# Splitting the last stores of a local-attention kernel, and issuing half of the very last one earlier

## The chip, the cores and the metric

One core of a Trainium2 chip. It has four compute engines (TensorE, VectorE, ScalarE and GpSimd: PE, DVE, ACT and POOL in the views) and SyncE (SP), which waits and issues transfers. Data are moved by 16 DMA engines; a packet of the trace is one piece that one of them moves, mostly one partition's share of a transfer (a unit's store shows 128 packets of 24,576 bytes, eight on each DMA engine). A semaphore is a counter that engines and transfers raise and that others wait for. The metric is device time in microseconds (us) of one execution; times named "of the trace" count from the start of the profiled span, which is about 2 us shorter than the device time (941.3 against 943.3).

## The reference, cut to what matters

```python
B, S, D, W = 4, 4096, 1536, 64            # float32 q, k, v and output, 100.66 MB each
# in windows of 64 rows, no row sees another window:
logits = einsum('bnwd,bnud->bnwu', q_w, k_w) * D ** -0.5
attn   = softmax(logits)
out    = einsum('bnwu,bnud->bnwd', attn, v_w)
```

Per input byte there is little arithmetic: each window is read once and written once.

## The kernel before

The 16,384 rows are worked off in N = 32 units of 512 rows; a partition holds four rows of a unit. GpSimd issues the loads (but for the first q, which SyncE loads) and the stores of units 0 to 30 on one queue; SyncE issues the very last store on its own queue. GpSimd's loads turn float32 into 16 bits on the way, so the packets count fewer bytes (253 MB) than HBM (403 MB); the page gives such a load of a unit 1536 KB, its store 3072. Three output buffers go round, so unit u may write its buffer when the store of unit u - 3 has landed.

```python
def store(u):                                          # GpSimd, one transfer of 3 MB
    nc.gpsimd.dma_start(
        out=rows(of, u * UR, SLOTS, SLOTS), in_=slots(outs[u % NO], 0, SLOTS, SLOTS)
    ).then_inc(d_o[u % NO], 16)
# ...
def told(ins, u, n, j, a):                             # n: row 0 to 3, j: third of the row
    if u == N - 1 and n >= 2:
        ins.then_inc(n_e[a], 1)                        # the last unit's rows 2 and 3 report here
    else:
        ins.then_inc(f_o[j][n], 1)
# ...
for u in range(1, N):                                  # GpSimd's stream
    hand_over("q", u, q16, m_q, g_q)                   # wait for the load, copy, request unit u + 2
    hand_over("k", u, k16, m_k, g_k)
    gp.wait_ge(m_q, u + 1)
    store(u - 1)
    hand_over("v", u, v16, m_v, g_v)
# SyncE, at the end:
for a in range(2):
    sy.wait_ge(n_e[a], 3)                              # VectorE's 3 and ScalarE's 3 tiles of rows 2, 3
sy.dma_start(
    out=rows(of, (N - 1) * UR, SLOTS, SLOTS), in_=slots(outs[(N - 1) % NO], 0, SLOTS, SLOTS)
).then_inc(d_l, 16)
# ... waits for all stores, then the end
```

The softmax here doesn't subtract the row's maximum and nothing guards it: scores larger than these inputs give would overflow.

## Time and profile before

| | before |
|---|---|
| time, median of 6 runs | 943.33 us (942.95 to 944.28) |
| span of the profiled run | 941.3 us |
| TensorE, ScalarE, GpSimd, VectorE busy | 68, 36, 35, 31% |
| packets of the GpSimd queue, share of 16 DMA engines | 99.7% |
| last store: issue, last packet's end, last semaphore count | 929.24, 939.46, 939.94 |

Read it as a kernel that streams: the DMA engines are full throughout (nines in the page's DMA row in all of the 40 slices but the last, which has a 7), so only the first and the last microseconds can hold idle DMA time.

How the packets lie on one DMA engine is in no view; it was worked out from the packet records of the trace, by chaining each packet to the one that ends where it starts. Two of the 16 chains of the tail, in us (an ordinary listing, not a view):

```
a typical engine:  ... 8 packets of the unit-30 store end 928.15 | idle 1.98 | 8 packets of the last store 930.14 to 937.50
the latest engine: ... 8 packets of the unit-30 store end 931.61 | idle 0.01 | 8 packets of the last store 931.62 to 939.46
                       (among the latter an 8 KB instruction fetch at 933.43, 0.31 long, the packet after it 1.18 instead of 0.91)
```

### The profile page before, as it was taken

The numbers are of one execution on the slowest core, as the hardware profiler recorded it, in microseconds if no ns is written. First come the engines' busy times: TensorE is split into PE (matmuls) and PEld (weight loads), VectorE is DVE, ScalarE is ACT, GpSimd is POOL, SyncE is SP. The second block draws the span as 40 slices with busy tenths as digits, with TensorE's granted clock in tenths as the row PEclk, the third lists the DMA queues.
The fourth block names the chain that finished last, engine by engine and source line by source line (L and its number), as shares of the span: only waits on it lengthen the run. The fifth ranks groups of instructions, "written<-read, shape, count | busy, mean of one in ns | idle before, by whom it ended". The sixth has DMA issues, their size and how long they took to land. (4 is left out here: it accounts for less than half of the span.)

```text
span 941.3 us, 13141 instructions
## 1 busy us (share of the span) xinstructions
PE 641.9 (68%) x5120; PEld 371.9 (40%) x3584; DVE 288.4 (31%) x517; ACT 336.0 (36%) x642; POOL 334.1 (35%) x225
## 2 busy tenths in 40 slices
PE   0877777666767767768676586676866767757673
PEld 0544444432444433444233442344533444323440
DVE  0233333332323333233322233222333223322232
ACT  0344444333333233333333333333334334233331
POOL 4244433344333342333423334333343333443220
PEclk9999999998889888797888999889789789888997
DMA  9999999999999999999999999999999999999997
GB/s 257 217 216 279 264 237 282 284 279 276 233 275 283 281 281 237 266 282 282 281 245 257 283 281 282 255 246 283 283 280 264 237 284 283 280 277 230 276 320 329
DMA packets 22540, 253.35 MB, mean 269 GB/s; under 512 B 2048, under 2 KB 2048, under 8 KB 10240
## 3 DMA queue, kind: packets, MB, share of 16 engines
q0 software_dynamic: 22240, 246.95, 99.7%
q1 hardware_dynamic: 288, 6.29, 1.7%
q14 instruction: 10, 0.08, 0.0%
q8 instruction: 2, 0.03, 0.0%
HBM read 301.99 MB, written 100.66 MB: 428 GB/s over the span
## 5 line engine op out<-in xcount | busy, mean ns | idle before, releaser
L164 PE MATMUL lt<-xq,xk 128*128 128x256 f16 x1536 | 203.3, 282 | 0.0
L300 POOL COPY v<-vl 128x3072 f32<-128x3072 f32 x31 | 85.2, 2748 | 278.3 <-DMA vl<-in_v_dram 278.3
L192 PEld LDWEIGHTS <-et 128*64 128x64 f16 x512 | 40.5, 131 | 331.6 <-issue 319.4
L152 PE MATMUL tp<-ident,k 128*128 128x128 f32 x768 | 124.9, 297 | 57.9 <-PEq L218 40.5
L164 PEld LDWEIGHTS lt<-xq,xk 128*128 128x128 f16 x1536 | 153.2, 100 | 27.3
L152 PE MATMUL tp<-ident,q 128*128 128x128 f32 x768 | 107.9, 285 | 80.1 <-DVE xq L228 55.8
L112 PE MATMUL sp<-ones,et 128*64 128x1 f16 x512 | 52.6, 178 | 147.8 <-PEq L218 130.6
L152 PEld LDWEIGHTS tp<-ident,q 128*128 128x128 f32 x768 | 85.9, 145 | 120.8 <-issue 120.7
L228 ACT COPY xk<-tp 128x512 f32<-128x512 f32 x96 | 59.6, 620 | 203.2 <-ACTq L218 203.2
L152 PEld LDWEIGHTS tp<-ident,k 128*128 128x128 f32 x768 | 96.0, 152 | 75.1 <-issue 73.1
L300 POOL COPY k<-kl 128x3072 f32<-128x3072 f32 x31 | 85.2, 2748 | 103.1 <-DMA kl<-in_k_dram 103.1
L245 DVE RECIPROCAL rs<-sp 128x1 f32<-128x1 f32 x128 | 21.4, 167 | 323.8 <-DVEq L218 323.2
L300 POOL COPY q<-ql 128x3072 f32<-128x3072 f32 x31 | 85.0, 2743 | 100.0 <-DMA ql<-in_q_dram 99.9
L228 DVE COPY xk<-tp 128x512 f32<-128x512 f32 x96 | 66.5, 693 | 168.2 <-DVEq L218 168.2
L112 PE MATMUL o<-v,et 128*64 128x512 f16 x768 | 117.7, 440 | 0.0
L279 ACT ACTIVATE out<-tp,rs 128x512 f32<-128x512 f32 x64 | 44.0, 687 | 177.4 <-ACTq L218 177.4
L269 ACT ACTIVATE et<-lt,zeros 32x128 f16<-32x128 f32 x256 | 92.0, 359 | 39.4 <-ACTq L218 36.1
L228 ACT COPY xq<-tp 128x512 f32<-128x512 f32 x96 | 56.3, 586 | 126.4 <-ACTq L218 126.4
L112 PE MATMUL tp<-v,et 128*64 128x512 f16 x512 | 100.2, 468 | 0.0
L256 DVE TENSOR_SCALAR out<-o,rs 128x512 f32<-128x512 f32 x128 | 90.4, 747 | 28.6 <-DVEq L218 28.6
L228 DVE COPY xq<-tp 128x512 f32<-128x512 f32 x96 | 66.1, 688 | 83.7 <-DVEq L218 83.7
L112 PE MATMUL lt<-v,et 128*64 128x512 f16 x256 | 64.5, 479 | 0.0
(21 smaller groups left out, 217.6 us busy)
## 6 DMA issues: line engine op xcount, KB each, us to landing
out_dram<-out POOLq DMA_DIRECT2D x31, 3072.0 KB, 61.6
ql<-in_q_dram POOLq DMA_DIRECT2D x31, 1536.0 KB, 54.9
kl<-in_k_dram POOLq DMA_DIRECT2D x31, 1536.0 KB, 54.9
vl<-in_v_dram POOLq DMA_DIRECT2D x31, 1536.0 KB, 54.9
out<-in_q_dram SPq DMA_DIRECT2D x1, 3072.0 KB, 16.7
out_dram<-out SPq DMA_DIRECT2D x1, 3072.0 KB, 10.7
k<-in_k_dram POOLq DMA_DIRECT2D x1, 1536.0 KB, 17.9
v<-in_v_dram POOLq DMA_DIRECT2D x1, 1536.0 KB, 24.3
```

Source lines behind the costliest of these rows:

```text
L112: return nc.tensor.add_instruction(mybir.InstMatmult(name=nc.get_next_instruction_name(), engine=PE, ins=[low(rhs), low(w)], outs=[low(o)] ...
L152: ins = nc.tensor.transpose(tps[g % 2][:, r, j, :], pairs[:, c * P : (c + 1) * P], ident[:, :])
L164: ins = nc.tensor.matmul(lts[h][:, r, :, :], lhsT=keys(c, h, r, w), rhs=queries(c, h, w), start=(c == 0 and w == 0 and r == 0), stop=(c == ...
L192: ld = nc.tensor.ldweights(w[h], tile_position=(0, P // H * h))
L228: copy(out=dst, in_=tps[g % 2][:, :, :, :]).then_inc(f_c[g % 4], 1)
L245: ve.reciprocal(out=rs[:, n : n + 1], in_=sp[:, n : n + 1]).then_inc(n_d, 1)
L256: ins = ve.tensor_scalar_mul(scaled(u, n, j), bank(n, j), scalar1=rs[:, n : n + 1])
L269: ins = sc.activation(ets[h][s, :, :, t], lts[h][s, :, :, t], EXP, bias=zeros[s, 0:1], scale=scale)
L279: ins = sc.activation(scaled(u, n, j), bank(n, j), COPY, bias=0.0, scale=rs[:, n : n + 1])
L300: gp.tensor_copy(out=dst[:, :, :].bitcast(FP32), in_=landing[x][u % NL][:, :, :].bitcast(FP32)).then_inc(c_l, 1)
```

## The change

Its intent: the last store should not wait for the whole last unit. Half of it goes out when rows 0 and 1 are done, and the stores of units 28 to 30 go out in halves as well, so that the end is made of smaller pieces. Core of the diff (the semaphore declarations and the changed wait counts of the buffers are cut):

```diff
     def store(u):
-        nc.gpsimd.dma_start(
-            out=rows(of, u * UR, SLOTS, SLOTS), in_=slots(outs[u % NO], 0, SLOTS, SLOTS)
-        ).then_inc(d_o[u % NO], 16)
+        n = 1 if u < N - 4 else 2
+        out, in_ = (
+            x[:, 0, :].rearrange("p (i d) -> p i d", i=n)
+            for x in (rows(of, u * UR, SLOTS, SLOTS), slots(outs[u % NO], 0, SLOTS, SLOTS))
+        )
+        for i in range(n):
+            nc.gpsimd.dma_start(out=out[:, i, :], in_=in_[:, i, :]).then_inc(d_o[u % NO], 16)
@@ SyncE, at the end
-        for a in range(2):
-            sy.wait_ge(n_e[a], 3)
-        sy.dma_start(
-            out=rows(of, (N - 1) * UR, SLOTS, SLOTS), in_=slots(outs[(N - 1) % NO], 0, SLOTS, SLOTS)
-        ).then_inc(d_l, 16)
+        last = rows(of, (N - 1) * UR, SLOTS, SLOTS)[:, 0, :]
+        for i, c in enumerate((1, 3)):
+            for a in range(2):
+                sy.wait_ge(n_e[a], c)
+            sy.dma_start(
+                out=last[:, 2 * i * D : 2 * (i + 1) * D],
+                in_=outs[(N - 1) % NO][:, 2 * i : 2 * (i + 1), :].rearrange("p r d -> p (r d)"),
+            ).then_inc(d_l[i], 16)
```

The compute engines keep their instructions and their order.

More of the change, by code (lines that the diff above doesn't have):

```diff
@@ L76 @@
     d_o = [sem(f"d_o{i}") for i in range(NO)]
-    d_l = sem("d_l")
+    d_l = [sem(f"d_l{i}") for i in range(2)]
     g_q, g_k, g_v = (sem(n) for n in ("g_q", "g_k", "g_v"))
@@ L284, in store, with stored @@
     def store(u):
-        nc.gpsimd.dma_start(
-            out=rows(of, u * UR, SLOTS, SLOTS), in_=slots(outs[u % NO], 0, SLOTS, SLOTS)
-        ).then_inc(d_o[u % NO], 16)
+        n = 1 if u < N - 4 else 2
[5 more added lines that the diff above has]
+            nc.gpsimd.dma_start(out=out[:, i, :], in_=in_[:, i, :]).then_inc(d_o[u % NO], 16)
+    def stored(u):
+        return 16 * (u // NO + 1) + (0 if u < N - 4 else 16)
     def request(x, u):
@@ L357 @@
         for u in range(NO, N):
-            sy.wait_ge(d_o[u % NO], 16 * (u // NO))
+            sy.wait_ge(d_o[u % NO], stored(u - NO))
             for a in range(2):
@@ L380 @@
             last = max(u for u in range(N - 1) if u % NO == i)
-            sy.wait_ge(d_o[i], 16 * (last // NO + 1))
-        sy.wait_ge(d_l, 16)
+            sy.wait_ge(d_o[i], stored(last))
+        for i in range(2):
+            sy.wait_ge(d_l[i], 16)
         lo, hi = min(s.num for s in sems), max(s.num for s in sems)
```

## The prediction

> **What bounds the kernel now.** I read the page first, its rows of utilisation and the DMA parts, because 32 units of the same work should show at once whether an engine or the DMA is full.
>
> ```profile
> DMA  9999999999999999999999999999999999999997
> q0 software_dynamic: 22240, 246.95, 99.7%
> q1 hardware_dynamic: 288, 6.29, 1.7%
> HBM read 301.99 MB, written 100.66 MB: 428 GB/s over the span
> ```
>
> No compute engine is over 68% busy; the 16 DMA engines are full from the first slice to the last but one. The inputs and the output must cross once (302 + 101 MB), and at the 428 GB/s of the last line that is the whole span of 941 us. So compute can only matter where the DMA engines run dry: at the start and at the end. The change touches only the end, so I next read the timeline of the last 40 us, with the waits of SyncE and the issues by line.
>
> ```profile
> 902.45 2.75 POOL L300 COPY k<-kl 128x3072 f32<-128x3072 f32 x1 [4.52 <-DMA kl<-in_k_dram]
> 905.82 0.54 POOL L285 DMA_DIRECT2D out_dram<-out  x1 [0.62 <-POOL k L300]
> 917.14 2.75 POOL L300 COPY v<-vl 128x3072 f32<-128x3072 f32 x1 [10.78 <-DMA vl<-in_v_dram]
> 926.22 0.69 ACT L279 ACTIVATE out<-tp,rs 128x512 f32<-128x512 f32 x1 [1.04 <-ACTq L218]
> 927.80 1.41 DVE L256 TENSOR_SCALAR out<-o,rs 128x512 f32<-128x512 f32 x2 [0.45 <-DVEq L218]
> 929.24 0.35 SPq L373 DMA_DIRECT2D out_dram<-out  x1
> SPq L382 <- DMA out_dram<-out: 10.3, 1, 10.3
> ```
>
> The last unit waits for its v until 917.14, computes until 929.21, its store is issued at 929.24, and SyncE then waits 10.3 us for the landing. That looks like a bare tail. The windows view says how bare:
>
> ```profile
> 917.00:928.00 11.00, 7.46 (x64) 1.31 (x16) 3.72 (x9) 4.73 (x10) 2.75 (x1) 0.84 0.99 427
> 928.00:930.00 2.00, 0.00 (x0) 0.00 (x0) 1.21 (x2) 0.49 (x1) 0.00 (x0) 1.00 0.29 123
> 930.00:937.00 7.00, 0.00 (x0) 0.00 (x0) 0.00 (x0) 0.00 (x0) 0.00 (x0) 0.60 1.04 440
> 937.00:939.50 2.50, 0.00 (x0) 0.00 (x0) 0.00 (x0) 0.00 (x0) 0.00 (x0) 0.50 0.09 39
> ```
>
> The last two columns are the mean DMA share and GB/s. Until 928 the engines still drain the stores of units 29 and 30, from 930 to 937 they move the last store, and there is a dent of 2 us between, where they are 29% busy. The dent is the target of the change. But the mean hides what decides: a transfer is shared by 16 engines and lands when the slowest is done. I therefore chained the trace's DMA packet records, engine by engine, from 919 us on (each packet starts where the one before it on its engine ends). Every engine carries 8 packets of 24,576 bytes per store, of 0.912 us each. In the dent, 12 engines idle about 1 to 2.4 us, one 0.18 us, and **three not at all**: two finish the last store at about 938.2 to 938.5 us, and the slowest finishes its stores on the GpSimd queue at 931.61, goes straight to its 8 packets of the last store, and ends at 939.46. The semaphore's last count comes at 939.94. The landings of the unit-30 store say the same without any chaining: its 16 counts come between 928.2 and 932.1 us, a spread of 3.9 us. The engine that sets the end never runs dry.
>
> [...]The trace agrees at the start, where packets of the SyncE load and of the GpSimd load alternate on each engine at 0.925 us apiece, with none lost. [...]issue start to first packet is 929.24 to 930.08, 0.84 us, and last packet to last count 0.48 us, so 1.3 us.
>
> **The change part by part.**
>
> First half of the last store: it now waits for one count from each of the two output engines among rows 2 and 3. These come when VectorE finishes its tile of row 2 (926.21 + 0.75 = 926.96) and ScalarE its first (926.22 + 0.69 = 926.91). So the issue moves from 929.24 to about 927.0, and first packets from 930.08 to about 927.9. The second half is issued at about 929.25, behind the first on the same queue; the first half holds each engine for 8 x 0.46 = 3.7 us, to 931.6 or later, so the second finds no gap. On the 12 fast engines the dent closes: about 1.6 us earlier, 937.5 to about 935.9. On the slowest engine the new packets at 927.9 only share with the unit-30 store that it still has to move until 931.6. Its sum of packets is unchanged, so its end is unchanged: **0 us**.
>
> Packets of 12,288 instead of 24,576 bytes, four units: a store packet takes 0.912 us, and a store's 4-byte semaphore packet 9 ns; I take those 9 ns as the fixed part, so two halves cost about 9 ns more than a whole. Each engine: 4 stores x (8 x 9 + 9 for the second semaphore packet) = 324 ns, all on the path: **+0.3 us**. For loads the fixed part is 22 ns (22-ns semaphore packets; 12 KB source packets 474 ns, 24 KB 926 ns); were that true of stores, it would be 4 x (8 x 22 + 22) = 0.8 us.
>
> Two issues by GpSimd for units 28 to 30: one more of 0.54 us each, 1.6 us in all. They lie in the waits for v (10.78 us in the line at 917.14), and no load remains to be requested behind them. Off the path: 0. The v of unit 31 queues behind the store of unit 28, so it lands about 0.08 us later and pushes the last unit's compute by that; hidden by the slow engine's backlog. Waits of SyncE on more counts: 0. Compute engines keep the same instructions in the same order.
>
> Sum: 943.34 + 0.3 = 943.6; I take off a little for the rival below: 943.4.
>
> **The rivals.** (a) *The dent closes for all.* If the end were set by the typical engine, 1.6 us would be saved, less 0.3: about 942.0. For it: the mean share of 0.29 and the 10.3 us wait. Against it: the slowest engine has no gap; the best that can be had with its lag unchanged is nothing. A partial form is plausible: part of the slow engine's lag is stretched packets (eight between 922 and 931 us took 0.916 to 0.987 instead of 0.912, 0.34 us in sum) and one 8 KB instruction fetch at 933.44 (0.31 us, and the packet after it 0.27 longer). If smaller packets stretch less, or the fetch falls elsewhere, up to 0.9 us goes away: 942.7. (b) *Interleaving costs.* The first packet after the change of queue took 1.46 and 1.73 us on the two other gapless engines, 0.5 to 0.8 more than usual. If every alternation cost that on the slow engine, its 8 or so alternations would add some 4 us: 947. Against it: the alternation at the start costs nothing, and the slow engine's own change of queue took 0.912. (c) *The tail becomes compute-bound* through a late v: no; it is 0.1 us of 12.
>
> **Range and chances.** The no-gain case with 0.3 to 0.8 us of packet cost gives 943.6 to 944.1; the partial gain gives 942.4 to 943.3; rival (a) 942.0. I hold the first at about 60%, the second at 30%. Repeats lie within 0.25 us, so 942.3 to 944.2 should hold 8 in 10. Two per cent is 19 us, more than the whole tail from the last issue to the end (12 us); only a mistake about the whole kernel could leave that band.
>
> **What would show it.** In the changed profile: two SyncE issues near 927.0 and 929.25; the dent of 928 to 930 gone (share near 1); store packets of 12,288 bytes at about 0.46 us; the 16 counts of the last transfer spread wider than now (2.2 us), fast engines near 936, the last still near 939.9; the two SyncE halves and the unit-30 store alternating on the slowest engine. I am wrong if the last count comes before 939, which would mean the slow engine's backlog was not fixed work, or if its packets grow well over 0.47 us.

Packets of two queues alternated at the start, at 0.925 us each. 943.34 measured before, +0.3 for the smaller packets and 0 for every other step gave 943.6, taken down to 943.4.

## More of the kernel before

The part of the page that sums up the packets is wanted later for comparison:

```profile
DMA packets 22540, 253.35 MB, mean 269 GB/s; under 512 B 2048, under 2 KB 2048, under 8 KB 10240
```

## The result, and the profile after

| | before | after |
|---|---|---|
| median of 6 runs | 943.33 us (942.95 to 944.28) | 943.38 us (943.15 to 943.77) |
| ratio | | 1.000, 95% interval 0.9987 to 1.0012 |

Ratios here are the mean time of one kernel's fast runs over that of the other's fast runs of the same rounds, so not quite the ratio of the medians quoted. A later set of five runs gave 943.30 against 943.29.

First the packet sum and the issues of the changed kernel (what, engine, operation, count, KB each, median us from issue to landing):

```profile
DMA packets 23116, 253.35 MB, mean 269 GB/s; under 512 B 2112, under 2 KB 2112, under 8 KB 10304
...
out_dram<-out POOLq DMA_DIRECT2D x28, 3072.0 KB, 61.6
...
out_dram<-out POOLq DMA_DIRECT2D x6, 1536.0 KB, 46.0
...
out_dram<-out SPq DMA_DIRECT2D x2, 1536.0 KB, 9.2
```

The bytes are the same, and there are 576 packets more: 4 stores x 128 more data packets and 4 x 16 more semaphore packets, just the split. Next, its timeline at the end (start, length, engine):

```profile
906.00 1.06 POOL L292 DMA_DIRECT2D out_dram<-out  x2 [0.60 <-POOL k L309]
...
917.43 2.75 POOL L309 COPY v<-vl 128x3072 f32<-128x3072 f32 x1 [10.37 <-DMA vl<-in_v_dram]
...
928.01 0.68 ACT L279 ACTIVATE out<-lt,rs 128x512 f32<-128x512 f32 x1
928.22 2.55 SPq L384 DMA_DIRECT2D out_dram<-out  x2
...
929.01 1.41 DVE L256 TENSOR_SCALAR out<-o,rs 128x512 f32<-128x512 f32 x2 [0.45 <-DVEq L218]
```

The second GpSimd issue (1.06 instead of 0.54 us) goes into the wait for v, as it should. SyncE issues the first half at 928.22, over 2 us before VectorE's last tile ends at 930.42. In this execution the last unit ended about 1.2 us later than in the profile before: its copy of v began 0.29 us later, and between 920 and 930 us TensorE was busy 8.38 us instead of 7.46, at a granted clock of 0.71 instead of 0.83. The windows of the tail (the two columns at the end are DMA share and GB/s):

```profile
928.00:930.00 2.00, 0.88 (x10) 0.00 (x0) 1.33 (x4) 1.38 (x3) 0.00 (x0) 1.00 0.76 320
930.00:937.00 7.00, 0.00 (x0) 0.00 (x0) 0.42 (x1) 0.00 (x0) 0.00 (x0) 0.69 0.95 401
937.00:939.50 2.50, 0.00 (x0) 0.00 (x0) 0.00 (x0) 0.00 (x0) 0.00 (x0) 0.50 0.10 44
```

The dent has gone from a share of 0.29 to 0.76 although compute was later. And yet the tail behind it, 937 to 939.5, is as long as before, with a tenth of the DMA engines at work. To see who they are, read the semaphore counts. Each transfer brings 16, one for each DMA engine, and the trace records when each came (2048 counts for the 128 transfers of the kernel before). For the last transfer of the last store, in us:

| kernel | issue (last one) | median engine | second to last | last |
|---|---|---|---|---|
| before | 929.24 | 937.84 | 938.86 | **939.94** |
| after | about 930.4 | 936.95 | 938.62 | **940.37** |

Put in order, fifteen of the counts come earlier than before, the median by 0.9 us. The sixteenth does not, and the kernel waits for it.

### The profile page after: what moved, and what is told of

Read it like the earlier page. It is cut to its first block, busy times and chain, and to the rows that moved or that the text cites. A ratio compares the mean times of both kernels' runs of the same rounds, so it can differ in the third digit from the quotient of the medians.

```text
span 941.7 us, 13147 instructions
## 1 busy us (share of the span) xinstructions
PE 645.0 (68%) x5120; PEld 373.9 (40%) x3584; DVE 288.5 (31%) x517; ACT 335.8 (36%) x642; POOL 336.2 (36%) x228
## 5 line engine op out<-in xcount | busy, mean ns | idle before, releaser
L152 PE MATMUL tp<-ident,q 128*128 128x128 f32 x768 | 109.8, 289 | 79.6 <-DVE xq L228 55.2
L112 PE MATMUL o<-v,et 128*64 128x512 f16 x768 | 119.9, 447 | 0.0
```

What stands on the lines that cost most here:

```text
L112: return nc.tensor.add_instruction(mybir.InstMatmult(name=nc.get_next_instruction_name(), engine=PE, ins=[low(rhs), low(w)], outs=[low(o)] ...
L152: ins = nc.tensor.transpose(tps[g % 2][:, r, j, :], pairs[:, c * P : (c + 1) * P], ident[:, :])
```

## The experiments

My theory: one DMA engine is so far behind that it never runs dry, and it alone sets the end. Its rival: the idle dent is on the path, closing it gains over a microsecond, and the smaller packets cost that much again. Ten kernels were run, each beside the kernel before.

### Which engine is late

```diff
@@ kernel before, SyncE, after the last store is issued
+        for m in range(1, 16):
+            c, at = 128 + 56 * m, 1024 * ((m - 1) // 6)
+            sy.dma_start(out=flat[m % 6][0:m, at : at + c], in_=qf[0:m, 0:c]).then_inc(d_t, 16)
```

(`flat` are the landing buffers, dead by then.)

> A mark, not a change: behind the last store of the kernel before, SyncE issues 15 small loads of 1 to 15 partitions, each with rows of its own size, into buffers that are dead by then. [...]My theory (one DMA engine is 1.5 to 2.2 us behind the other 15 and sets the end) expects the chain that ends the last store last to carry 0 to 15 marks, and to be one single chain; if the lag belongs to the instruction fetches, the 8 KB fetch packets lie on the same chain. The rival (the end is set by all engines alike) expects the last-store ends of all chains within 0.5 us.

Measured: a single run of 947.68 us (state unknown; the marks make it longer, which is meant). The last store's counts came at 938.79 us for the median engine, at 939.12 for the last but one, at 940.80 for the last. The mark packets of six of the 15 sizes, starts in us:

```
m=3   938.67 938.76 938.82
m=4   938.64 938.72 938.81 938.88
m=5   938.71 938.79 938.88 938.94                 939.95
m=6   938.49 938.78 938.86 938.95 939.01          940.02
m=7   938.39 938.56 938.86 938.93 939.03 939.09   940.10
m=8   938.53 938.55 938.65 938.94 939.02 939.11 939.17   940.18
```

Each transfer of 5 or more partitions has one straggler, about a microsecond behind its fellows, and those of 1 to 4 have none. So one engine is late, and by these marks transfers of five or more partitions reach it and those of four or fewer don't. I call it the fifth, or engine 4, counting from 0 in the order in which engines come in as transfers grow; that is a name only, for which number it has on the chip is not shown. The 8 KB instruction fetch lies on the same chain, as it does in the kernel before.

### Delaying the last store

```diff
@@ kernel before, ScalarE, after its last tile (3 or 6 times)
+            sc.activation(xq[:, i, :], xk[:, i, :], COPY, bias=0.0, scale=1.0).then_inc(n_e[1], 1)
@@ SyncE
-            sy.wait_ge(n_e[a], 3)
+            sy.wait_ge(n_e[a], 3 + 3 * a)      # 3 + 6 * a
```

> The kernel before with 3 idle activations of some 0.6 us on ScalarE between its last output tile and the issue of the last store, so the issue moves from 929.24 to about 930.4 (+1.1 us). Theory (slowest engine has its backlog until 931.6, so up to 1.5 us of delay are free): end moves by 0 to 0.2 us. Rival (the dent is on the path): end moves by +1.1 us. If the rival's arrow holds, closing the dent should have gained.

> The same with 6 idle activations: the issue moves to about 932.3 (+3.0 us). Theory: the slowest engine's backlog covers the first 1.5 us, so the end moves by about +1.5 us. Rival: +3.0 us.

Measured: 943.66 us with three and 945.36 us with six idle activations, against 943.18 for the kernel before in the same rounds (ratios 1.0005, interval 0.9991 to 1.0018, and 1.0019, interval 1.0005 to 1.0033). The timelines show the issue of each; first three, then six:

```profile
929.38 1.66 ACT L285 ACTIVATE xq<-xk 128x512 f32<-128x512 f32 x3
931.14 0.35 SPq L378 DMA_DIRECT2D out_dram<-out  x1
```

```profile
929.70 3.21 ACT L285 ACTIVATE xq<-xk 128x512 f32<-128x512 f32 x6
933.02 0.35 SPq L378 DMA_DIRECT2D out_dram<-out  x1
```

Set the counts against the issues:

| kernel | issue | median engine | last |
|---|---|---|---|
| before | 929.24 | 937.84 | 939.94 |
| three activations | 931.14 | 939.75 | 940.54 |
| six activations | 933.02 | 941.64 | 942.40 |

The issue came 1.90 us later in the first step, not the 1.1 expected, because the last unit itself ran later in this execution. The median engine follows it fully, by 1.91 us; the last one by 0.60 only. In the second step the issue is 1.88 us later, the median engine 1.89, and now the last one 1.86. So about 1.3 us of delay are free (1.90 less 0.60) and every microsecond beyond costs one. That is the theory's shape, with 1.3 us for the 1.5 foretold, and it rules out that the dent was on the path: what a delay of 1.3 us doesn't cost, an advance doesn't gain. The third row shows the other part of the lag: there the late engine has no backlog left and begins its share of the last store with the others, at about 933.9, and yet it ends 0.76 us behind the median. On its chain lies the instruction fetch, at 937.85, with three stretched packets beside it. So, as an estimate, of its 2.1 us in the kernel before 0.6 to 0.8 belong to the fetch in the tail and the rest to the backlog.

### A load of four partitions, or of five

```diff
@@ kernel before, SyncE, ahead of its waits for the last unit (m = 4 or 5)
+        sy.wait_ge(c_l, copies[0])
+        for x in "qk":
+            sy.dma_start(
+                out=landing[x][0][:, :, :].bitcast(FP32).rearrange("p s d -> p (s d)")[0:m, :],
+                in_=qf[0 : 2 * m].rearrange("(p r) d -> p (r d)", r=2),
+            ).then_inc(d_t, 16)
```

> The kernel before, with two loads of 4 partitions x 12,288 bytes on SyncE's queue at about 920 us, into dead buffers: 2 packets more, some 0.95 us[...]. The marks of the run which_engine put the late chain on engine 4 (marks of 5 and more partitions, none of 4 and fewer). Theory: these engines' last store landed by 938.9 at the latest, 1.1 us ahead of engine 4, so the end moves by 0 to 0.2 us. Rival (any added work counts): +0.2 us in the mean, or +0.95 us.

> The same with 5 partitions, so the same 0.95 us on engine 4 too, in all one partition more. Theory: the last count comes 0.95 us later than in the kernel before (939.94 to about 940.9) and the time grows by 0.9 us. If engine 4 did not set the end: as with 4 partitions.

(Engine 4 is a name in the same sense. That a load of four partitions leaves it out is taken from the marks. Which engines carry that load instead ("these engines"), no run shows.)

Measured: 943.56 us with four partitions (942.93 to 943.73) and 944.40 us with five (944.07 to 944.72); the kernel before 943.27 in these rounds. No run of the one reaches into the range of the other. Against the kernel before, the ratios are 1.0000 (interval 0.9985 to 1.0016) and 1.0010 (0.9995 to 1.0026), so it is the comparison of the two that tells. The last stores were issued within 0.1 us of each other, in the runs with four and with five:

```profile
930.65 0.38 SPq L380 DMA_DIRECT2D out_dram<-out  x1
```

```profile
930.57 0.38 SPq L380 DMA_DIRECT2D out_dram<-out  x1
```

The median engine's count came at 939.28 and 939.21, but the last at 940.56 and 941.56. The fifth engine's 0.95 us go into the end one for one (1.00 us between these two counts); four partitions' load, of which it carries nothing, does not show in the time (ratio 1.0000). One thing missed the expectation: with four, the last count came 0.62 us later than in the kernel before, not 0 to 0.2. In that execution the late engine finished its packets of the GpSimd queue at 932.23 instead of 931.62, without an added load, so single profiles differ by that much; with five it carries the two added packets (0.46 us each) and finishes them at 933.22. With this the theory is shown from both sides: a delay of the whole last store is free up to about 1.3 us; let the load reach engine 4 as well, and the end moves.

### What a packet costs

```diff
@@ changed kernel
-        n = 1 if u < N - 4 else 2
+        n = 4                                   # all 31 stores of GpSimd
@@ stored(u)
-        return 16 * (u // NO + 1) + (0 if u < N - 4 else 16)
+        return 64 * (u // NO + 1)
```

> The changed kernel with all 31 GpSimd stores (not the last 3) split, and into four one-row transfers instead of two: store packets of 6,144 bytes, 32 per engine and store, 4 semaphore packets. Prices the packet by itself. At 9 ns fixed per store packet: 31 x (24 x 9 + 3 x 9) = 7.5 us more than the kernel before, all on the DMA engines that set the pace: about 951 us. At 22 ns (the fixed part of loads): 31 x 27 x 22 = 18 us: 962 us. At nothing: 943.4 us.

Measured: 946.74 us (946.62 to 947.21) against 943.18, ratio 1.0036, interval 1.0023 to 1.005. That is 3.56 us for 31 x 27 more packets on each engine, or 4.3 ns for each, half of the smaller guess. The trace agrees: the v of unit 31 begins to land at 917.55 instead of 913.65, 3.9 us later behind 29 split stores, 5.0 ns a packet. So does the spacing: whole packets of a store mostly start 908 ns apart, quarter packets 230 or 231, so three more packets cost about 14 ns, 4.7 each. So the split in the changed kernel, 4 x 9 packets, costs 0.15 to 0.2 us.

### Each part alone

```diff
@@ changed kernel, "last pair only": the GpSimd stores stay whole
-        n = 1 if u < N - 4 else 2
+        n = 1
@@ changed kernel, "three split only": SyncE's last store is again one transfer, behind n_e[a] >= 3
```

> The changed kernel with the three GpSimd stores left whole, so only the last store goes in two. Theory: the dent closes on the fast engines (last counts of 15 engines near 936.5), engine 4 still ends near 939.9: within 0.2 us of the kernel before. Rival (closing the dent gains and the split stores eat it): 1.3 us faster than the kernel before.

> The other part alone: stores of units 28 to 30 in two transfers, the last store whole and issued once as before. From the run all_split4 a further store packet costs about 4.3 ns (3.56 us over 31 x 27 packets), so 3 x 9 x 4.3 ns = 0.1 us: the same as before. The rival sum of the prediction, 9 ns, gives 0.25 us; neither can be told from the times, only from the spacing of the packets.

Measured: 943.18 us and 943.16 us, against 943.27 for the kernel before (ratios 1.0000 and 0.9999, intervals within 0.9985 and 1.0013). The first is the clean case of the dent, for compute ran early in its profile (clock 0.83, as before). Its issue and its windows:

```profile
927.49 2.56 SPq L384 DMA_DIRECT2D out_dram<-out  x2
```

```profile
928.00:930.00 2.00, 0.15 (x2) 0.00 (x0) 1.41 (x2) 0.69 (x1) 0.00 (x0) 1.00 0.97 406
930.00:937.00 7.00, 0.00 (x0) 0.00 (x0) 0.00 (x0) 0.00 (x0) 0.00 (x0) 0.52 0.85 358
937.00:939.50 2.50, 0.00 (x0) 0.00 (x0) 0.00 (x0) 0.00 (x0) 0.00 (x0) 0.50 0.13 54
```

The dent is gone (share 0.97), the median engine is done at 936.25, 1.6 us earlier than before, and the last count comes at 940.02. The 1.6 us have become idle time of fifteen engines behind their work instead of idle time ahead of it. In the second kernel the last count comes at 940.16. The times alone would barely exclude the rival, for the interval reaches down to its 1.3 us (0.14%); the last count does, which the rival needs at about 938.6. Since neither part alone moves the end, they don't cancel each other, and the rival falls.

### Taking work off the late engine

```diff
@@ changed kernel: the second half of the unit-30 store only
+        cut = (0, 5, 60, 65, 120, 125, 128)
-            nc.gpsimd.dma_start(out=out[:, i, :], in_=in_[:, i, :]).then_inc(d_o[u % NO], 16)
+            for lo, hi in parts:                # the pieces between the cuts
+                nc.gpsimd.dma_start(out=out[lo:hi, i, :], in_=in_[lo:hi, i, :]).then_inc(d_o[u % NO], 16)
```

> The changed kernel, with rows 2 and 3 of the unit-30 store, which GpSimd issues at 906 us, in six transfers of 5, 55, 5, 55, 5 and 3 partitions instead of one of 128. [...]the last count at about 938.3 instead of 940.37, the time some 2 us below the changed kernel, 941.3. If the transfers are spread otherwise, engine 4 may carry more than eight of the packets and the end comes later by up to 2 us. Rival (engine 4 isn't the limit): no change.

> The changed kernel once more, on the chip and in the rounds of the run steer, for its times (943.2 to 943.6) and for a second look at its tail: last counts of 14 engines near 936.5, engine 4 near 940.2.

Measured: 947.62 us (947.02 to 949.58), ratio 1.0052, interval 1.0038 to 1.0066; the changed kernel again 943.30 us, ratio 1.0003. The attempt failed: it costs 4.3 us, more than even the bad case that I had foreseen. The counts of the last transfer spread from 937.09 to 944.36, with two engines beyond 944. Some of the store's packets took 1 to 2 us instead of 0.46, so this isn't only a matter of which engine got how many. Why they stretch, and how these pieces were dealt out, stays open. The repeat of the changed kernel gave a median count of 936.66 and a last of 940.06. No run gave a version that beats both kernels beyond the noise.

## Why the prediction was right

Predicted 943.4 us, measured 943.38. That the two agree to 0.02 us is luck: the working gave 943.6, from which 0.2 was taken off by feel, and repeats of the kernel before lie up to 1.3 us apart (942.95 to 944.28), not within 0.25 as the prediction had it from three runs. What was foretold is no change, and for that the mechanism counts. By its own steps:

- **The slowest engine gains nothing:** right. Its last count is at 940.37 and 940.06 in two profiles of the changed kernel, 939.94 before; delay and added load show that it alone sets the end.
- **Fast engines about 1.6 us earlier:** right where compute ran as before (936.25 against 937.84), 0.9 and 1.2 us in the two profiles of the changed kernel, whose last unit ran later.
- **+0.3 us for smaller packets:** the mechanism is right, the size was off by half. The term "9 ns for each packet", taken from the length of a semaphore packet, is 4.3 to 5.0 ns by measurement, so 0.15 to 0.2 us. Lengths overstate it, because records on one engine overlap: a whole packet is 912 ns long, but the next starts after 908. The guess of 22 ns is out.
- **Second issues of GpSimd off the path:** right, 1.06 us inside a wait of over 10. (That no load is requested behind them holds for units 29 and 30 only; the v of unit 31 is requested behind the store of unit 28, at 862. Its first count came 0.08 us later than before, as foretold, its last 0.28.)
- **Rival (a), the dent closes for all, and its partial form:** refuted for the full form by the last pair alone. The partial form, less lag on engine 4, did not come: the fetch came again, at 933.36, and the last count was not earlier.
- **Rival (b), alternation costs 4 us:** the cost did not come. But the picture behind it was wrong: on the late engine the packets did not alternate from the arrival of the first half on, as they do at the start (0.925 us each). In the changed kernel, other engines began the first half at about 929.1; the late one ran six more packets of the GpSimd queue, 2.8 us, before its first of SyncE's at 931.98. As the sum of its packets is the same in either order, nothing in the time hung on it.
- **Spread of the last transfer wider than 2.2 us:** right, 3.55 us, and 3.53 in the repeat.
- **The 428 GB/s as proof that DMA bounds the kernel:** circular, for that figure is the bytes divided by the span. What carries the step is the row of the DMA share, nines in all slices but the last.

What is not explained is why engine 4 is late. It carries an instruction fetch in the tail (0.31 us, and 0.27 on the packet after it). The spread between the first and the last count of a transfer grows over the run, from 1.7 to 1.8 us in the landings from 19 to 78 us (2.7 in the very first) to 3.9 in the store of unit 30. From about 450 to 730 us the last count is within 0.2 us of the one before it; then it falls back by 0.07 to 0.25 us a unit, to 1.37 us at the store of unit 30. That growth comes unit by unit and not at the fetches on record (697 and 878 us), so they don't explain it.

## What to carry to other kernels

Here a transfer landed when the slowest of its DMA engines was done: fifteen counts of the last store were in by 938.86 us, the sixteenth came at 939.94, and SyncE's wait lasted until then. So before closing a gap in the mean DMA share, look at the counts of its semaphore one by one: if the latest engine has no gap (here 0.01 us, against 1.98 on a typical one), starting earlier gains nothing (here 943.38 us against 943.33). A cheap test is the reverse of the change: delay the step on purpose, and if that is free, as the first 1.3 us were here, hastening it is worth nothing. Work added once with and once without that engine then shows whether it is the limit (here a last count of 941.56 with it, 940.56 without).
